# Retention values of two heads by seven products, with a DRAM round trip, and a reordered core sequence

## The chip, the cores and the metric

The kernel runs on one core of a Trainium2 chip. The metric is device time in microseconds (us) of one execution. TensorE does the matmuls, VectorE and ScalarE the elementwise work, GpSimd some of it, and SP, ScalarE and GpSimd issue DMA transfers.

## The reference

Two layers of a trunk: gated delta net with a convolutional FFN, then retention with the same FFN, each step closed by a layer norm. The change lies in the second layer's mixer, for 1024 tokens, 1024 features, 4 heads, keys of 256 and values of 512 per head, chunks of 128 tokens:

```python
def retention(h, w_in, w_out):
    H, dk, dv, C = RET_HEADS, RET_DK, RET_DV, RET_CHUNK          # 4, 256, 512, 128
    q, k, v, gate = jnp.split(h @ w_in, [H * dk, 2 * H * dk, 2 * H * dk + H * dv], axis=-1)
    ...                                                          # q, k rotated by position
    scores = jnp.einsum('bhncd,bhnmd->bhncm', q, k) * dmask[None, :, None]
    intra = jnp.einsum('bhncm,bhnmv->bhncv', scores, v)
    def step(state, inp):
        q_n, k_n, v_n = inp
        o = jnp.einsum('bhck,bhkv->bhcv', q_n, state) * xi[None, :, :, None]
        state = (state * gamma_c[None, :, None, None]
                 + jnp.einsum('bhck,bhcv->bhkv', k_n * zeta[None, :, :, None], v_n))
        return state, o
    _, inter = lax.scan(step, jnp.zeros((b_, H, dk, dv), F32), xs)
    o = _unchunk_heads(intra + jnp.moveaxis(inter, 0, 2))
    o = _standardize(o, 1e-6).reshape(b_, s, H * dv)             # each row of 512 to mean 0, variance 1
    o = o * jax.nn.silu(gate.astype(F32))
    return o.astype(h.dtype) @ w_out
```

## The kernel before

Most float32 matmuls are made of three: each operand is split into a high and a low part in a rounded format (`split`: ScalarE copies the high part, VectorE subtracts it for the low part), and low x high, high x low and high x high are added up in PSUM. One 128x512 result over 128 features is thus three matmuls (`mma`, `mm3`).

PSUM has eight banks of 128x512: four "acc", two "mm", two "sc". SBUF tiles come from tags with fixed numbers of buffers: "qkv" 20 (128x512 each), "aux", "cv" and "lane" 4, "auh" and "hTb" 8, "wr", "wh", "wl" and "xT" 2.

Big products run as Strassen-Winograd: the tokens (two halves) and features (two halves) of the activations give four blocks 11, 12, 21, 22 and four sums T1 to T4, and seven products of half size replace eight. `strassen` does so for the q, k and gate projections of the layer, and leaves its activation blocks (`B`) in SBUF: 11 and 21 in "hTb", T1 and 22 in "hTa", T2 in "aux", T3 and T4 in "qkv".

The value projection of each head, in the kernel before, is plain: `ret_v(h, half)` multiplies half the tokens (4 tiles of 128, one "acc" bank each) by 8 blocks of 128 features: 96 matmuls. It then splits each of the four results into a pair of "qkv" tiles, or waits for room there (`take`). It is called for head 0 halves 0 and 1, then head 1, and so on.

A core (`core(h)`) walks the 8 chunks of a head. Per chunk: two state products (kz by v, three matmuls each, into an "sc" bank, added to the state by VectorE), the next chunk's scores and key transposes (`ret_front`, "mm" bank), then the output product (scores by v, and q by state, "sc" bank). `ret_back` takes the output's statistics on VectorE, the power -0.5 on GpSimd, normalises the row (tile "on"), transposes it on TensorE, multiplies it with the gate loaded from DRAM ("gt", giving "ot") and stores it to DRAM (`od`), from chunk 4 on also in sums and differences with the earlier half ("op", made by GpSimd), as the output projection's blocks.

The output projection (`proj_gen`, started by `start_out`) is a seven-product scheme too; its first product reads eight blocks of `od`, two per head. Block j may start when the event `("ob", j // 2)` of head j // 2 stands, which is set after chunk 3 of that core; the last two blocks are the seventh and eighth, of head 3.

The order on TensorE in this stage is written by a planner (`run`): generators yield times to wait or events; the planner keeps a clock from the cost of each matmul, always advances the ready generator of lowest number, and pins the matmuls in that order. Cores have -1.0, `ret_back` -0.1, the filler `ret_fill` 0: it yields the value projection and then the first two products of the output projection, in groups of three matmuls, whenever no core is ready. The constants `RL` are the planner's latencies: "q" 5.9 us for loading q and k, "f" 3.35 after the first front, "p" 0.55, "c" 2.75 after an output product, "o" 4.42 from a transposed row to the output projection's block. Everything that is not pinned is placed by the framework's scheduler, each engine and queue running its instructions in order.

Of the kernel before, what the change touches and what calls it, by code (L numbers as in the profile page):

```python
# [15 lines left out]
P = 128  # L16
# [17 lines left out]
def trunk_kernel(ctx: ExitStack, tc, A):  # L34
# [1882 lines left out]
    B = strassen(h0, xts, sc_r, sh_r, [gate_item(0), gate_item(2)] + mixed, ("hTa", "aux", "qkv", "qkv", "hTa"), True)  # L1917
    hT = [h0, []]
# [7 lines left out]
    hT[1] = build_hT("hTa", xlo, sc_r, sh_r, range(4)) + B["22"]  # L1926

    def ret_v(h, half):
        accs = acc4()
        for kp in range(4):  # L1930
            wh, wl = load_w(A["ret_wv"][h, kp])
            if (h, half, kp) == (RH - 1, 1, 3):
                yield after_ev(("qk", h))
                start_out()
            for kk in range(2):
                kt = kp * 2 + kk
                hl = hT[half][kt]
                ns = slice(kk * 4, kk * 4 + 4)
                for t in range(4):
                    ts_ = slice(t * P, (t + 1) * P)  # L1940
                    pm(accs[t], hl[1][:, ts_], wh[:, ns], start=(kt == 0), stop=False)
                    pm(accs[t], hl[0][:, ts_], wl[:, ns], start=False, stop=False)
                    pm(accs[t], hl[0][:, ts_], wh[:, ns], start=False, stop=(kt == KT - 1))
                    yield 0.0
            if kp % 2 or h == RH - 1:
                bg_step()
        for t in range(4):
            yield from take("qkv", 2)
            vv = two("qkv", F32R, "vv")
            split(vv[0], vv[1], accs[t])  # L1950
            va[h].append(vv)
# [23 lines left out]
    def core(h):  # L1975
        yield after_ev(("rv", h, 0), ("core", h - 1))
        if h == 1:
            bg_ada(1, 2, "row")
        q, k = load_qk(h, 0), load_qk(h, 1)
        emit(("qk", h))  # L1980
        St = None
        yield RL["q"]
        r = ret_front(h, 0, q, k)
        yield RL["f"]
        for n in range(NCH):
            if n == 4:
                yield after_ev(("rv", h, 1))
            vh, vl = va[h][n]
# [25 lines left out]
            give("qkv", 2)  # L2014
# [3 lines left out]
        emit(("core", h))  # L2018

    def ret_back(h, n, po):  # L2020
# [9 lines left out]
        anchor["on"] = dve.tensor_scalar(on, po, mv[:, 0:1], mv[:, 3:4], ALU.subtract, ALU.mult)  # L2030
# [33 lines left out]

    def load_qk(h, j):
# [8 lines left out]
    RL = {"v": 2.57, "q": 5.9, "f": 3.35, "p": 0.55, "c": 2.75, "b": 3.21, "o": 4.42}  # L2074
    va = [[] for _ in range(RH)]

    def ret_fill():
        for h in range(RH):
            for half in range(2):
# [39 lines left out]
    run([(0.0, ret_fill())] + [(-1.0, core(h)) for h in range(RH)])  # L2119
# [104 lines left out]
```

## Time and profile before

| what | value |
|---|---|
| time, median of 3 runs (lowest, highest) | 2871.21 us (2867.52, 2874.64) |
| the profiled execution's own time, and its span | 2872.47 us, 2870.7 us |
| TensorE, VectorE, ScalarE, GpSimd busy over the span | 97%, 76%, 45%, 17% |
| granted TensorE clock | 0.994 |
| matmul records | 13594 |
| HBM read, written | 346.86 MB, 115.87 MB |
| DMA engines' mean rate | 162 GB/s |

In the lines below, a window's row gives the busy microseconds (and count) of TensorE matmul, its weight load, VectorE, ScalarE and GpSimd, then the granted clock, the DMA share and GB/s. A row of the chain gives start, duration and what the time went to. A matmul's duration includes its way through the pipeline; its cost in a dense stretch is the distance from one start to the next. In a timeline row, square brackets hold the engine's idle time ahead of the instruction and what ended it.

### The profile page before, as it was taken

Reading aid. Unit: us, or ns where it says so; the run is one execution under the profiler, and the core shown is the slowest. Engines: PE = TensorE matmul, PEld = TensorE weight load, DVE = VectorE, ACT = ScalarE, POOL = GpSimd, SP = SyncE. Lnnn points to the kernel's source line nnn. Section 1 sums busy time; section 2 is a strip of 40 time slices with the busy share of each in tenths; the row PEclk is TensorE's granted clock in tenths of the full one; section 3 lists DMA queues with packets and bytes.
Section 4 is the critical chain, followed back from the end, with each engine's and each line's share of the span. In section 5 each row is a group of like instructions: output and inputs, shape, how many; then the busy total and the mean of one; then the engine's idle time right before and its main releaser. Section 6 shows DMA issues by size and latency. Waiting matters only on the chain.

```text
span 2870.7 us, 38939 instructions
## 1 busy us (share of the span) xinstructions
PE 2785.2 (97%) x13594; PEld 2277.0 (79%) x13594; DVE 2183.3 (76%) x3874; ACT 1294.0 (45%) x2377; POOL 500.2 (17%) x517
## 2 busy tenths in 40 slices
PE   8999999999999999999999999999999999999997
PEld 6787878877787788887888887777787778888886
DVE  6887678676788888778677656666788887777869
ACT  3763465344644444546433342222344644444443
POOL 0411321000023233100000002333301033332001
PEclk9999999999999999999999999999999999999999
DMA  8323242174254555945343364665854253444853
GB/s 279 101 90 115 92 140 92 61 250 150 99 180 168 192 183 172 336 126 180 128 147 119 121 204 153 200 196 160 275 194 147 74 194 132 143 139 161 320 150 118
DMA packets 254292, 465.31 MB, mean 162 GB/s; under 512 B 24400, under 2 KB 81104, under 8 KB 254096
## 3 DMA queue, kind: packets, MB, share of 16 engines
q1 hardware_dynamic: 219776, 407.50, 43.0%
q10 hardware_dynamic: 31488, 46.15, 4.4%
q0 software_dynamic: 2832, 9.18, 0.8%
q8 instruction: 107, 1.75, 0.2%
q14 instruction: 89, 0.73, 0.1%
HBM read 346.86 MB, written 115.87 MB: 161 GB/s over the span
## 4 chain that ended last, share of the span: by engine, by line
PE 56%; DVE 21%; DMA 11%; ACT 6%; issue 5%; POOL 1%; SPq 0%; ACTq 0%; DVEq 0%; POOLq 0%
PE acc L747 10%; PE acc L1340 5%; PE acc L110 4%; PE sc L747 4%; PE acc L111 4%; PE acc L112 4%; PE sc L1340 3%; PE acc L1636 3%; DMA mvw<-in_ada_w 3%; DVE o L1787 3%; DMA wr<-in_ffn_up 2%; PE mm L747 2%; DVE wb L90 2%; DVE qkv L507 2%; DVE mm L1394 1%
## 5 line engine op out<-in xcount | busy, mean ns | idle before, releaser
L747 PE MATMUL acc<-hT,wh 128*128 128x512 f32 x960 | 299.7, 393 | 0.0
L1636 PE MATMUL acc<-bb,ab 128*128 128x512 f32 x984 | 229.8, 392 | 6.5 <-DVE ab L90 4.1
L89 ACT ACTIVATE ab<-ar 128x512 fp32r<-128x512 f32 x210 | 131.1, 629 | 217.0 <-PE mm L316 55.1
L1636 PEld LDWEIGHTS acc<-bb,ab 128*128 128x128 f32 x984 | 183.0, 188 | 48.6 <-DVE ab L90 4.7
L747 PEld LDWEIGHTS acc<-hT,wh 128*128 128x128 f32 x960 | 182.5, 190 | 35.6
L1340 PE MATMUL acc<-T,wb 128*128 128x512 f32 x840 | 202.0, 389 | 0.4 <-DVE wb L90 0.4
L90 DVE TENSOR_TENSOR ab<-ar,ab 128x512 fp32r<-128x512 f32 x210 | 148.7, 715 | 68.5 <-ACT ab L89 68.1
L747 PE MATMUL acc<-hT,wl 128*128 128x512 f32 x480 | 197.3, 411 | 1.2 <-ACT sq L531 0.7
L89 ACT ACTIVATE wb<-mm 128x512 fp32r<-128x512 f32 x216 | 124.4, 597 | 163.0 <-DVE mm L1394 150.1
L1340 PEld LDWEIGHTS acc<-T,wb 128*128 128x128 f32 x840 | 157.5, 188 | 33.8 <-ACT o L1788 1.1
L90 DVE TENSOR_TENSOR wl<-wr,wh 128x1024 fp32r<-128x1024 f32 x95 | 118.6, 1249 | 74.3 <-ACT wh L89 72.6
L1818 POOL TENSOR_TENSOR o<-o 128x512 f32<-128x512 f32 x80 | 119.0, 1496 | 270.1 <-DVE o L1810 167.9
L90 DVE TENSOR_TENSOR wb<-wr,wb 128x512 fp32r<-128x512 f32 x162 | 114.2, 706 | 65.7 <-ACT wb L89 65.6
L89 ACT ACTIVATE wh<-wr 128x1024 fp32r<-128x1024 f32 x95 | 100.6, 1060 | 138.3 <-PE acc L747 61.4
L1787 DVE SCALAR_TENSOR_TENSOR o<-g,vc,o 128x512 f32<-128x512 f32 (+2 forms) x176 | 152.2, 875 | 8.9 <-ACT o L1782 7.7
L90 DVE TENSOR_TENSOR wb<-mm,wb 128x512 fp32r<-128x512 f32 x216 | 144.5, 682 | 7.4 <-ACT wb L89 7.4
L89 ACT ACTIVATE wb<-wr 128x512 fp32r<-128x512 f32 x162 | 101.2, 626 | 95.5 <-PE acc L1340 28.8
L1394 DVE TENSOR_TENSOR mm<-wr 128x512 f32<-128x512 f32 x108 | 83.9, 777 | 71.4 <-DMA wr<-in_ffn_up 58.2
L747 PE MATMUL acc<-wh,hT 128*128 128x512 f32 x384 | 134.3, 412 | 2.1 <-DVE vv L90 2.1
L1410 ACT ACTIVATE pc<-acc 128x512 f32<-128x512 f32 x143 | 84.4, 591 | 111.8 <-PE acc L1340 63.6
L252 DVE SCALAR_TENSOR_TENSOR ada<-mvw,e,ada 128x512 f32<-128x512 f32 x140 | 105.8, 755 | 24.0 <-DMA mvw<-in_ada_w 23.8
L110 PE MATMUL acc<-T,wb 128*128 128x512 f32 x292 | 114.9, 394 | 3.6 <-DVE wb L90 3.3
(677 smaller groups left out, 7356.2 us busy)
## 6 DMA issues: line engine op xcount, KB each, us to landing
wr<-in_ffn_up SPq DMA_DIRECT2D x92, 512.0 KB, 3.9
mvw<-in_ada_w SPq DMA_DIRECT2D x80, 512.0 KB, 4.3
ad<-o SPq DMA_DIRECT2D x154, 256.0 KB, 2.3
ar<-ad SPq DMA_DIRECT2D x154, 256.0 KB, 4.2
Br<-in_ffn_down SPq DMA_DIRECT2D x88, 256.0 KB, 5.2
wr<-in_ret_wv SPq DMA_DIRECT2D x32, 512.0 KB, 3.6
ar<-od SPq DMA_DIRECT2D x56, 256.0 KB, 4.5
wr<-in_gdn_wqkv SPq DMA_DIRECT2D x24, 512.0 KB, 3.9
```

The lines of the kernel that those rows point to most:

```text
L89: anchor["sp"] = act.activation(dst_h, src, AF.Copy)
L90: eng.tensor_tensor(dst_l, src, dst_h, ALU.subtract)
L110: mm(acc, wl[:, k], hl[0], start=first, stop=False)
L111: mm(acc, wh[:, k], hl[1], start=False, stop=False)
L112: mm(acc, wh[:, k], hl[0], start=False, stop=last)
L252: dve.scalar_tensor_tensor(a, wr[:, kk], e[:, k:k + 1], a, ALU.mult, ALU.add)
L747: pq(pe.matmul(out, lhsT, rhs, start=start, stop=stop), cost or COST[out.shape[-1]])
L1340: return pe.matmul(*a, skip_group_check=True, **kw)
L1394: dve.tensor_tensor(t, x, y, op)
L1636: return pe.matmul(*args, skip_group_check=True, **kw)
L1787: dve.scalar_tensor_tensor(tv, gv[:, c0 - j:c1 - j], w[:, 2 - j:3 - j], tv, ALU.mult, ALU.add)
L1818: (dve if fp == 0 else pool).tensor_tensor(o[d], o[x], o[y], op)
```

## The change

Three things are changed.

1. Values of heads 0 and 1 are computed ahead of the planner's run by seven products (`values_01`) on the blocks that `strassen` left, and stored to DRAM (`vd`). During the run `fetch_v` loads them back at most two chunks ahead. The second half of the plain activations (`hT[1]`) is built inside this step.
2. The filler now holds only the values of heads 2 and 3, by token halves: both heads' first half, then both heads' second half; head 2's second half goes into "hTb". Core h + 1 starts after the event that core h now sets at chunk 6, and its q and k are loaded at chunk 5. The output projection's start waits for the event `("ob", 1)`.
3. The normalisation of each row moves from VectorE to ScalarE: VectorE makes minus mean times power (128x1), ScalarE scales and shifts.

```diff
+    def values_01():
+        W = A["ret_wv"]
...
+        def operand(p, j):
+            if p == 0:
+                src = first[j]
+            elif p == 1:
+                src = load(0, 1, j)
+            elif p == 2:
+                src = keep[j] = load(1, 0, j)
+                dve.tensor_tensor(src, src, load(1, 1, j), ALU.add)
+            elif p == 3:
+                src = keep[j]
+                dve.tensor_tensor(src, src, first[j], ALU.subtract)
...
+            t = tl(("wh", "wl")[(4 * p + j) % 2], [P, 2, HALF], F32R, name="wb")
+            split(t[:, 0], t[:, 1], src)
+            return t[:, 0], t[:, 1]
...
+        def put(h, n, c):
+            vv = two("qkv", F32R, "vv")
+            split(vv[0], vv[1], c)
+            for i in range(2):
+                act.dma_start(vd[h, n, i], vv[i].bitcast(F32))
...
+        for p, nm in enumerate(("11", "21", "T1", "T2", "22", "T3", "T4")):
+            fresh = p in (0, 1, 2, 6)
+            if p == 0:
+                X = acc4()
+            elif fresh:
+                Z = [sc_tile(), sc_tile(), mm_tile(), mm_tile()]
+            if p == 5:
+                hT[1] = build_hT("hTa", xlo, sc_r, sh_r, range(4)) + B["22"]
+            accs = X if p in (0, 3, 5) else Z
+            ws = []
+            for j in range(4):
+                while len(made) < min(4 * p + j + 4, len(steps)):
+                    made.append(operand(*steps[len(made)]))
+                ws.append(made[4 * p + j])
+                if j < 2:
+                    for t in range(4):
+                        mma(accs[t], t, B[nm][j], ws[j], fresh and j == 0, False, pe.matmul if fresh else mm_on)
+            if p in (0, 2, 3, 5):
+                part[p] = four("lane" if p == 2 else "xT")
+            for t in range(4):
+                for j in (2, 3):
+                    mma(accs[t], t, B[nm][j], ws[j], False, j == 3, pe.matmul if fresh else mm_on)
+                if p in part:
+                    act.activation(part[p][t], accs[t], AF.Copy)
+                if p in (1, 4, 5, 6):
+                    c = part[{1: 0, 4: 3, 5: 2, 6: 5}[p]][t]
+                    dve.tensor_tensor(c, accs[t], c, ALU.add)
+                    put(p // 5, t + (4 if p in (4, 5) else 0), c)
...
-    hT[1] = build_hT("hTa", xlo, sc_r, sh_r, range(4)) + B["22"]
+    values_01()
...
             if (h, half, kp) == (RH - 1, 1, 3):
-                yield after_ev(("qk", h))
+                yield after_ev(("ob", 1))
                 start_out()
...
         for t in range(4):
-            yield from take("qkv", 2)
-            vv = two("qkv", F32R, "vv")
+            if (h, half) != (2, 1):
+                yield from take("qkv", 2)
+            vv = two("qkv" if (h, half) != (2, 1) else "hTb", F32R, "vv")
...
     def core(h):
-        yield after_ev(("rv", h, 0), ("core", h - 1))
+        yield after_ev(("rv", h, 0) if h > 1 else ("vf", h, 0), ("core", h - 1))
         if h == 1:
             bg_ada(1, 2, "row")
-        q, k = load_qk(h, 0), load_qk(h, 1)
-        emit(("qk", h))
+        if not h:
+            qk[0] = load_qk(0, 0), load_qk(0, 1)
+            emit(("qk", 0), RL["q"])
+        q, k = qk[h]
         St = None
-        yield RL["q"]
+        yield after_ev(("qk", h))
         r = ret_front(h, 0, q, k)
         yield RL["f"]
         for n in range(NCH):
-            if n == 4:
+            if n == 5 and h < RH - 1:
+                qk[h + 1] = load_qk(h + 1, 0), load_qk(h + 1, 1)
+                emit(("qk", h + 1), RL["q"])
+            if n == NCH - 2:
+                emit(("core", h))
+            if n == 4 and h > 1:
                 yield after_ev(("rv", h, 1))
+            if h < 2:
+                yield after_ev(("vf", h, n))
...
-            give("qkv", 2)
+            if h != 2 or n < 4:
+                give("qkv", 2)
+            used[0] += 1
...
-        anchor["on"] = dve.tensor_scalar(on, po, mv[:, 0:1], mv[:, 3:4], ALU.subtract, ALU.mult)
+        dve.scalar_tensor_tensor(mv[:, 2:3], mv[:, 0:1], -1.0, mv[:, 3:4], ALU.mult, ALU.mult)
+        act.activation(on, po, AF.Identity, bias=mv[:, 2:3], scale=mv[:, 3:4])
...
+    def fetch_v():
+        for m in range(2 * NCH):
+            yield lambda: m < used[0] + 2
+            yield from take("qkv", 2)
+            vv = two("qkv", F32R, "vv")
+            for i in range(2):
+                sp.dma_start(vv[i].bitcast(F32), vd[m // NCH, m % NCH, i])
+            va[m // NCH].append(vv)
+            emit(("vf", m // NCH, m % NCH), RL["l"])
...
     def ret_fill():
-        for h in range(RH):
-            for half in range(2):
+        for half in range(2):
+            for h in range(2, RH):
                 yield from ret_v(h, half)
...
-    run([(0.0, ret_fill())] + [(-1.0, core(h)) for h in range(RH)])
+    run([(0.0, ret_fill()), (-2.0, fetch_v())] + [(-1.0, core(h)) for h in range(RH)])
```

More of the change, by code (lines that the diff above doesn't have):

```diff
@@ L2017, in core @@
             St, r = Sn, rn
-        emit(("core", h))
+        emit(("done", h))
     def ret_back(h, n, po):
@@ L2063, in ret_back @@
             (pool if n == NCH - 1 and h == RH - 1 else sp).dma_start(blk(nm), d)
+    used, qk = [0], {}
+    def fetch_v():
[7 more added lines that the diff above has]
+            emit(("vf", m // NCH, m % NCH), RL["l"])
     def load_qk(h, j):
@@ L2072, in load_qk @@
         return out
-    RL = {"v": 2.57, "q": 5.9, "f": 3.35, "p": 0.55, "c": 2.75, "b": 3.21, "o": 4.42}
+    RL = {"v": 2.57, "q": 5.9, "f": 3.35, "p": 0.55, "c": 2.75, "b": 3.21, "o": 4.42, "l": 4.0}
     va = [[] for _ in range(RH)]
     def ret_fill():
-        for h in range(RH):
-            for half in range(2):
+        for half in range(2):
+            for h in range(2, RH):
                 yield from ret_v(h, half)
```

27 lines of the change are left out of this document (added).

## The prediction

> **What bounds the kernel now.** I read the page's head first, then the stage that the change touches (from the last product of the input projections, 1702.3 us, to the end of the output projection's second product, 2082.0 us) by windows, then the chain of work in one chunk, then the rows of the operations that are added or removed.
>
> ```profile
> span 2870.7 us, 38939 instructions
> PE 2785.2 (97%) x13594; PEld 2277.0 (79%) x13594; DVE 2183.3 (76%) x3874; ACT 1294.0 (45%) x2377; POOL 500.2 (17%) x517
> ```
> ```profile
> 1640.00:1700.00 60.00, 59.44 (x262) 48.90 (x262) 43.55 (x69) 22.06 (x38) 0.00 (x0) 1.00 0.53 168
> 1702.30:2082.00 379.70, 371.79 (x1671) 287.64 (x1670) 242.59 (x430) 103.12 (x174) 119.54 (x132) 1.00 0.63 197
> 2020.00:2062.00 42.00, 39.95 (x176) 29.49 (x174) 28.61 (x58) 12.75 (x26) 12.48 (x17) 1.00 0.80 254
> ```
>
> TensorE bounds the kernel. The first window is the stage of seven-product input projections just ahead (TensorE 99%, VectorE 73%, ScalarE 37%), the second the stage of the change (98%, 64%, 27%), both at full clock. So a matmul taken away is worth its issue interval, as long as nothing else then runs out. One chunk of a retention core, from the chain that ended last:
>
> ```profile
> 1749.28 0.65 PE mm L750 x6
> 1749.93 0.69 PE acc L747 x3
> 1750.62 2.42 PE sc L747 x7
> 1753.04 3.44 PE acc L747 x15
> 1756.48 1.36 PE sc L747 x6
> 1757.84 0.44 PE mm L747 x4
> 1758.28 0.65 PE mm L750 x6
> ```
>
> The chunk takes 9.00 us. The "acc" pieces are filler (the value projection): 18 matmuls in 4.13 us, 0.229 each. The other 4.87 us are the core itself. Filler hides the core's waits, above all the one behind the 2.42 us output product: its rows must be normalised before their PSUM bank (two "sc" banks for all) takes the next chunk's second state product.
>
> ```profile
> 1753.08 0.70 DVE L2022 BATCH_NORM_STATS2 rst<-sc 128x6 f32<-128x512 f32 x1 [0.24 <-PE sc L747]
> 1754.91 0.81 DVE L2030 TENSOR_SCALAR on<-sc,mv 128x512 f32<-128x512 f32 x1 [0.73 <-POOL mv L2026]
> ```
>
> That is 1753.04 to 1755.72, 2.7 us, under 3.44 us of filler. What the change does to the amount of filler is therefore the question.
>
> **The change, part by part.**
>
> *Matmuls.* Values of heads 0 and 1 cost 2x2x8x4x3 = 384 matmuls; seven products of 4x4x3 = 48 cost 336. 48 x 0.229 = **-11.0 us**. The sixteen transposes for the second half of hT stay (moved to the sixth product).
>
> *Stalls that go.* In the old stage the filler has one set of four accumulators, drained between value halves with no core running beside it:
>
> ```profile
> 1728.08 0.62 issue
> 1728.70 0.69 DVE vv L90
> ...
> 1806.22 1.37 DVE vv L90 x2
> ...
> 1808.23 0.68 DVE vv L90
> ...
> 1810.05 0.61 DVE vv L90
> 1810.70 7.14 PE acc L747 x30
> 1818.50 3.43 PE acc L747 x15
> ...
> 1887.44 1.37 DVE vv L90 x2
> ...
> 1889.44 0.68 DVE vv L90
> ...
> 1891.17 0.69 DVE vv L90
> ...
> 1977.77 0.69 DVE vv L90
> ```
>
> The chain puts 7.4 us on these drains; TensorE still ran the old core's last products under part of them, so I count a little under half. The new stage alternates two sets of banks, and its four remaining drains fall inside chunks, where the core's own matmuls cover them: **-3.5 us** (bounds -7.4 and 0).
>
> *The new stage of seven products.* 76.9 us of TensorE. VectorE: 28 splits, 16 operand sums, 16 result sums, 16 value splits, 4 hT splits = 80 at 0.69 (the vv row) = 55 us, 72%; the first window runs 99% dense at 73%. ScalarE: 68 passes at 0.6, plus 32 stores issued at 0.33:
>
> ```profile
> 1651.09 0.33 ACTq L1899 DMA_DIRECT2D qd<-pc  x1
> ```
> ```profile
> L89 ACT ACTIVATE vv<-acc x32: 577/598/602, 1724.4 to 2012.2; 128x512 fp32r<-128x512 f32 x32
> ```
>
> That is 51 us, 67%, against 37% in that window, and every second store waits on ScalarE's queue for VectorE's low half, with the next operand's high half behind it. Operands are made four blocks ahead (four times 2.75 us), but only four "wb" buffers exist, so the lead is two blocks, 5.5 us. Also, only four of the twenty "qkv" buffers are free until T3 is spent, so the third value pair of the second product waits for the store of the first (3-4 us by the store rows below). Cost between 0.6 us (the first window's share of idle) and 6 us (two late operands of a lead lost); I take **+2**, nearer the window, which has the same structure. Weight loads fall (7 MB for 8), and 8 MB of stores with 8 MB of reloads come. At a DMA share of 0.5 to 0.6 they fit; the reloads stand on SP's queue some 12 us ahead of use by the two-chunk rule in fetch_v, priced at nothing; if SP stands still for over 12 us they show as a wait of "sc" matmuls for vv.
>
> *The order of the cores.* Now a core's q and k are loaded at chunk 5 and the next core starts at chunk 6. The old gap between cores held 30 + 15 filler matmuls (the rows at 1810 and 1818), 10.6 us. From core 1 on, the next core's first chunk now lies between the old one's last two (after core 0 it waits for the reloaded values). Both share two "sc" banks and two "mm" banks, and the second state product of the new core waits for the normalised row of the old one's chunk 6: 2.7 us less one filler group (0.69) and the first state product (0.68), 1.3 us. Then chunk 7's square products stand on GpSimd ahead of the new core's power:
>
> ```profile
> 1787.25 4.15 DMA od<-ot
> ...
> 1791.46 0.74 POOL ot L2062
> ```
> ```profile
> 1792.75 0.81 DVE L2030 TENSOR_SCALAR on<-sc,mv 128x512 f32<-128x512 f32 x1 [2.56 <-POOL mv L2026]
> ...
> 1813.45 0.69 DVE L2051 TENSOR_TENSOR ot<-mm,gt 128x512 f32<-128x512 f32 x1 [2.81 <-DMA od<-op]
> ```
>
> In this jam (a store, then GpSimd, then the row) the row waited 2.56 us in place of 0.73, 1.8 late against a slack of 1.4 (3.44 + 0.68 - 2.7): 0.4 us of TensorE, which stays. Two overlapped boundaries at 1.3, and one such 1.8 with no filler over it, make **+4** (bounds 0, where filler lies in between, and 3 x 4.15 = 12).
>
> *ScalarE normalises the row.* A 128x1 step on VectorE (0.15, as its neighbours) and a ScalarE pass (0.60) replace 0.81: 0.66 us per chunk off VectorE, 0.60 onto ScalarE, the row 0.1 to 0.2 us later through one more hand-over. Under 3.44 us of filler that is nothing; without filler it is 0.15 a chunk. ScalarE's queue now waits for GpSimd's power too, with kz and sThl behind it, as VectorE's did. The anchor "on" falls away with VectorE's row, and with it the order that holds the projection's T1 weight sums behind the last row:
>
> ```profile
> 2058.76 3.03 DVE L1515 TENSOR_TENSOR Bw<-Br,Bw 128x512 f32<-128x512 f32 x4
> ```
>
> They may now come earlier, ahead of rows or splits: bounds -3 and +3. Together **0**.
>
> *Filler.* The planner's order can be followed by hand from its own costs; a filler group is three matmuls. Groups there are: 128 (values of heads 2 and 3) and 24 (six of eight blocks of the output projection's first product), 152 in all, before its seventh block must wait for core 3's fourth chunk ("ob", 3). Used: 20 before core 0's first chunk, 46 from there to core 1's, 42 to core 2's second chunk, 30 for its chunks 1 to 5, 6 in the overlap, 6 in core 3's chunk 1: 150. **Filler ends in chunk 2 of core 3.** Before, 256 + 24 groups stood against the same cores, and the seventh block came late:
>
> ```profile
> 2025.87 0.60 PE L750 MATMUL mm<-cst,on 128*128 128x128 f32 x4
> ...
> 2046.87 4.00 PE L747 MATMUL acc<-bb,ab 128*128 128x512 f32 x15
> ```
>
> The first row turns row 3 of core 3; the seventh block begins in the second row, 21 us on, when its data had long been there. Now chunk 3 lacks 2.1 us of cover (2.8 to the released bank, less the first state product's 0.68), chunk 2 lacks 1.4 (one group is left). In chunk 4 the planner allows 4.42 us from the transposes of row 3 to the seventh block (the constant "o"), then puts its matmuls into TensorE's order ahead of chunk 5. Behind them on TensorE stand chunks 5 to 7. The true way is: product with the gate, store, load, split. (The other new wait, start_out behind ("ob", 1), is reached in core 2, when core 1's first half is long stored: 0.)
>
> ```profile
> od<-ot ACTq DMA_DIRECT2D x48, 128.0 KB, 3.6
> ...
> ar<-od SPq DMA_DIRECT2D x39, 256.0 KB, 5.3
> ```
> ```profile
> DMA to landing us min/median/max: 1.8/3.7/7.9
> ```
> ```profile
> DMA to landing us min/median/max: 2.7/5.3/7.9
> L89 ACT ACTIVATE ab<-ar x25: 615/632/634, 1996.4 to 2099.1; 128x512 fp32r<-128x512 f32 x25
> L90 DVE TENSOR_TENSOR ab<-ar,ab x24: 674/682/1227, 1997.0 to 2097.0; 128x512 fp32r<-128x512 f32 x24
> ```
>
> By medians 0.69 + 3.6 + 5.3 + 0.63 + 0.68 = 10.9 us; chunk 4's output product covers 2.4, so TensorE stands 8.5. By the shortest landings (1.8, 2.7) 6.5, so 4.1. Starved time: 1.4 + 2.1 + 4.1 to 8.5 = 7.6 to 12.0; I take **+10**, the middle: no value weights are loaded any more then, but the stretch has a DMA share of 0.80 (third window). The bounds are 0, if the cores reach this point with filler left, and 15, with the longest landing of the load (7.9).
>
> A page bears on the load and store. The Trainium skill, "DMA: Bandwidth & Descriptors", section "Anatomy of one DMA", gives about 2.0 us fixed plus bytes at 436 GB/s for transfers that GpSimd issues (these come from SP and ScalarE), an estimate here of 2.3 us for 128 KB and 2.6 us for 256 KB. By it the gap would be 4.5 in place of 8.5, starvation 8.0, and the sum -0.5 with that in place of +10. The trace's medians, 3.6 and 5.3, are longer than the page gives, so the rows carry the sum.
>
> *Sum.* -11.0 - 3.5 + 2 + 4 + 0 + 10 = **+1.5 us**. The profiled execution took 2872.47 us (span 2870.7), 1.3 above the median of 2871.21; so 2872.7 on the runs' scale. About 0.3% (8.6 us) is what a measurement of this kernel tells from no change.
>
> **The rivals.**
>
> *Faster: the filler suffices.* If core 3 is reached later in the filler's supply, or the seventh block's data come inside other work, starvation is 0 to 2 and boundaries 1. For it: TensorE was 98% dense with 18 matmuls a chunk, and the new run has exactly 576 = 32 x 18 filler matmuls. Against it: 120 of them are locked behind ("ob", 3). -11.0 - 3.5 + 2 + 1 + 1 = -10.5: 2861.
>
> *Slower: the ring of four "cv" buffers at the overlaps.* Chunk 7 of one core and chunk 0 of the next need op, gate row and result at once; VectorE stands at the result's product until a store has landed (2.81 in the row at 1813), now with a core behind it that has no filler. One store (3.6) and one such wait (2.81) at each of three boundaries are 19 us for my 4: +16.5, 2888. It decides (beyond 8.6) from 3.7 us per boundary. For it: the old gap of 10.6 us between cores cleared that ring, and it is gone. Against it: chunk 0 needs no op buffer.
>
> *The operands bind in the seven products.* Every second block late by 0.7 us on ScalarE's queue: 14 x 0.7 = 10 in place of 2: 2881. Against it stands the window ahead.
>
> **Chances.** Forecast 0.50; filler suffices 0.27; ring 0.15; operands 0.08. Forecast's own range 2865 to 2880. The first and third rival reach beyond 0.3% on their sides: faster 0.27, same 0.50, slower 0.23. The range takes the faster rival's centre and half of the slower ones: 2859 to 2884.
>
> **What would show it.** Right: 48 fewer matmuls; the seven products in about 79 us; TensorE's gaps in the last core, chunks 2 to 4, with its longest wait for the seventh block's split; rows from ScalarE at about 0.6 us; no wait of "sc" for reloaded vv. Wrong: filler still present in core 3's chunk 4; long gaps at the ends of cores 0 to 2; "wb" splits releasing TensorE in the seven products; or a time moved outside 1702 to 2082, where nothing is edited.

## The result, and the profile after

The changed kernel took 2888.48 us in the median of 4 runs (2885.99 to 2889.99), the kernel before 2870.24 beside it: a ratio of 1.0065, 95% interval 1.0048 to 1.0081. The change made the kernel slower by 18.7 us (the ratio times 2870; the medians differ by 18.2). Forecast was 2872.7, with a range of 2859 to 2884.

The head of the page of the changed kernel, then its windows (the columns are the stretch, its length, busy time and instructions of TensorE, weight loads, VectorE, ScalarE and GpSimd, the granted clock, DMA share and GB/s):

```profile
span 2887.1 us, 39162 instructions
PE 2781.2 (96%) x13546; PEld 2269.8 (79%) x13546; DVE 2188.2 (76%) x3918; ACT 1327.8 (46%) x2437; POOL 496.5 (17%) x517
...
1700.40:2098.80 398.40, 369.40 (x1624) 282.20 (x1624) 250.63 (x478) 135.53 (x233) 113.33 (x132) 0.98 0.72 232
...
1700.40:1780.00 79.60, 79.60 (x360) 65.96 (x360) 48.57 (x75) 41.60 (x69) 0.00 (x0) 1.00 0.62 214
...
1793.00:1820.00 27.00, 24.60 (x113) 18.60 (x112) 19.89 (x42) 8.22 (x15) 7.96 (x7) 1.00 0.93 318
1820.00:1864.00 44.00, 44.00 (x200) 33.32 (x199) 24.73 (x54) 13.29 (x23) 15.82 (x20) 1.00 0.75 245
1864.00:1886.00 22.00, 16.72 (x70) 13.21 (x69) 11.36 (x21) 4.21 (x7) 9.14 (x11) 0.84 0.80 234
1886.00:1920.00 34.00, 34.00 (x159) 26.52 (x158) 22.35 (x45) 11.02 (x18) 7.57 (x9) 1.00 0.80 251
1920.00:1958.00 38.00, 32.53 (x147) 23.21 (x146) 22.05 (x50) 9.85 (x17) 20.45 (x25) 1.00 0.75 225
...
1980.00:1996.00 16.00, 12.36 (x45) 8.20 (x44) 13.11 (x24) 5.89 (x11) 2.57 (x4) 0.89 0.77 263
1996.00:2022.00 26.00, 22.39 (x105) 16.05 (x104) 16.82 (x41) 7.98 (x15) 13.11 (x17) 1.00 0.59 170
2022.00:2040.00 18.00, 17.31 (x79) 12.90 (x78) 10.33 (x21) 3.46 (x6) 8.40 (x10) 1.00 0.58 177
2040.00:2060.00 20.00, 13.03 (x41) 8.21 (x40) 9.96 (x24) 6.08 (x11) 3.62 (x4) 0.84 0.71 223
2060.00:2098.80 38.80, 37.86 (x168) 29.07 (x167) 28.35 (x49) 14.60 (x27) 18.18 (x23) 1.00 0.80 251
```

The 48 matmuls are gone (13546 for 13594). The whole loss lies in the stage forecast: 398.4 us where the window of before had 379.7, that is +18.7. (Ahead of the stage the profiled execution is 1.9 us shorter than the one of before, and behind it 0.4, so the two spans are 16.4 us apart; runs of the kernel before alone differ by 7.) Take a window's length less TensorE's busy time as idle. The seven products (the second window) have none. The rest has 29.0 us, all in a few places: 2.4 as core 0 starts, 5.3, 5.5 and 3.6 at the three boundaries between cores (1864, 1920, 1996), 3.6 at 1980, and 0.7 + 7.0 + 0.9 in the last core. Before had 379.70 - 371.79 = 7.9 in all. The stretches between are dense at 44.00 of 44.00 and 34.00 of 34.00: cores with filler are as good as they were.

The clock is the other part. The records of the granted clock show half speed for 17.1 us of the stage (6.83 from 1876.0, 3.41 from 1988.6, 6.83 from 2053.5) against 3.4 before. What ran then took twice its time. TensorE stood idle in 2.0 us of the 17.1, so half of the 11.7 us more in which it worked is lost: 5.8. The account: -11.0 for the matmuls, +21.1 of idle time, +5.8 of clock are +15.9 of the 18.7. Most of the other 2.8 is a matter of counting: a matmul's record lasts 0.389 us and its cost is 0.229, so a gap takes 0.16 us more than its idle time. The stage has 22 gaps of over 0.25 us, and had 8 before; 14 times 0.16 is 2.2 us, an estimate. Counted with these 0.16, the gaps named below are 5.4 us (5.3 of idle time), 4.75 (4.6) and 2.1 (1.95).

Now the chain of waits at five of these places (start, duration, what): core 0's second chunk, the boundary of cores 0 and 1, the boundary of cores 1 and 2, core 2's modulations, and the seventh block of the output projection.

```profile
1794.77 8.29 DMA xg<-xs
...
1806.25 5.54 DMA xg<-xg
...
1811.89 0.70 DVE Sr L2098
...
1867.12 4.27 DMA xg<-xs
...
1871.56 1.24 POOL xg L2211
...
1874.66 0.72 POOL op L2161
1875.39 0.52 POOL mv L2124
...
1875.93 0.68 DVE mv L2128
...
1876.69 0.79 ACT on L2129
...
1877.53 1.65 PE sc L747 x3
...
1880.03 1.28 PE mm L750 x6
...
1944.10 2.79 DMA od<-op
...
1947.10 0.70 DVE ot L2150
...
1947.85 0.66 PE mm L750 x4
...
1981.05 4.67 DMA ar<-od
...
1986.40 0.69 DVE ab L90
...
1987.68 0.76 DVE ada L252
...
1988.58 2.00 PE mm L274 x2
...
2050.30 3.88 DMA ar<-od
...
2054.20 0.64 ACT ab L89
...
2054.87 0.70 DVE ab L90
...
2055.62 1.65 PE acc L747 x3
```

The second place is the largest gap of the stage. GpSimd's queue is in order. On it stand a gain row (the residual row times the layer's gain plus its bias, lines 2211 and 2212), whose load takes 4.27 us and keeps GpSimd waiting, then sums and differences of core 0's last chunks (L2161), and behind them the power (L2124) without which core 1's row can't be normalised. The row holds a PSUM bank, and TensorE stands 5.4 us. The rows after this gap show the clock: six transposes take 1.28 us, which took 0.65 at full clock before. The first place shows the same row by another way: core 0's state "Sr" takes a "lane" buffer that the gain row leaves only when its store has landed (5.54). The third place has no gain row on its chain: VectorE stands at the gated product until a store of "op" has landed (2.79), and transposes of TensorE stand behind it. That is the way of the prediction's second rival, the ring of "cv" buffers, which hold "op", "gt" and "ot".

The waits of GpSimd for these loads, in the kernel before (first row) and after (second row; engine, line, what it waited for: us, times, longest):

```profile
POOL xg L2100 <- DMA xg<-xs: 410.9, 15, 355.4
```
```profile
POOL xg L2211 <- DMA xg<-xs: 54.6, 15, 5.7
```

Before, one wait was 355.4 us, on an engine with nothing to do; the other fourteen make 55.5 us. After, all fifteen make 54.6. So the wait did not grow; the experiments ask whether its cost did.

### The profile page after: what moved, and what is told of

Its sections match the earlier page's. It is cut to its first block, busy times and chain, and to the rows that moved or that the text cites. A ratio compares the mean times of both kernels' runs of the same rounds, so it can differ in the third digit from the quotient of the medians.

```text
span 2887.1 us, 39162 instructions
## 1 busy us (share of the span) xinstructions
PE 2781.2 (96%) x13546; PEld 2269.8 (79%) x13546; DVE 2188.2 (76%) x3918; ACT 1327.8 (46%) x2437; POOL 496.5 (17%) x517
## 4 chain that ended last, share of the span: by engine, by line
PE 61%; DVE 18%; DMA 10%; ACT 5%; issue 4%; POOL 1%; SPq 1%; ACTq 0%; DVEq 0%; POOLq 0%
PE acc L747 7%; PE acc L1340 6%; PE acc L1636 4%; PE acc L110 4%; PE acc L111 4%; PE acc L112 4%; PE sc L1340 3%; PE sc L747 3%; PE mm L747 2%; DVE o L1787 2%; DVE qkv L507 2%; DMA mvw<-in_ada_w 2%; DMA wr<-in_ffn_up 2%; PE sc L110 2%; PE sc L112 2%
## 5 line engine op out<-in xcount | busy, mean ns | idle before, releaser
L1636 PE MATMUL acc<-bb,ab 128*128 128x512 f32 x984 | 230.3, 392 | 10.8 <-DVE ab L90 8.0
L1340 PE MATMUL acc<-T,wb 128*128 128x512 f32 x840 | 202.0, 389 | 0.4 <-DVE wb L90 0.4
L90 DVE TENSOR_TENSOR wl<-wr,wh 128x1024 fp32r<-128x1024 f32 x79 | 97.9, 1241 | 51.1 <-ACT wh L89 50.7
L89 ACT ACTIVATE wh<-wr 128x1024 fp32r<-128x1024 f32 x79 | 83.7, 1061 | 90.5 <-PE acc L341 47.3
L110 PE MATMUL acc<-T,wb 128*128 128x512 f32 x292 | 114.8, 393 | 2.9 <-DVE wb L90 2.8
L112 PE MATMUL acc<-T,wb 128*128 128x512 f32 x292 | 114.4, 392 | 0.0
```

The lines of the kernel that those rows point to most:

```text
L89: anchor["sp"] = act.activation(dst_h, src, AF.Copy)
L90: eng.tensor_tensor(dst_l, src, dst_h, ALU.subtract)
L110: mm(acc, wl[:, k], hl[0], start=first, stop=False)
L112: mm(acc, wh[:, k], hl[0], start=False, stop=last)
L1340: return pe.matmul(*a, skip_group_check=True, **kw)
L1636: return pe.matmul(*args, skip_group_check=True, **kw)
```

## The experiments

The theory at the start of them: the cores are short of cover in particular places (boundaries, starved last core), through waits that can be named. The rivals: the 8 MB of stores and reloads crowd the DMA queues; the row on ScalarE is too slow; the filler is short as such. Differences below are in ratios to the kernel before, which ran beside each; 0.001 is 2.9 us.

**One part undone at a time.**

```diff
-        dve.scalar_tensor_tensor(mv[:, 2:3], mv[:, 0:1], -1.0, mv[:, 3:4], ALU.mult, ALU.mult)
-        act.activation(on, po, AF.Identity, bias=mv[:, 2:3], scale=mv[:, 3:4])
+        anchor["on"] = dve.tensor_scalar(on, po, mv[:, 0:1], mv[:, 3:4], ALU.subtract, ALU.mult)
```


> The changed kernel with the row normalised by VectorE again (third part undone, its anchor back). Changed kernel: 2888.5 us; before: 2870.2. Theory 'row' (ScalarE took 0.78 us for a row and not 0.60, and one more hand-over, each chunk's bank later by 0.5 us wherever filler lacks): 2880 or less. Theories 'boundaries' and 'block' (the stalls come from the order of the cores and from the output projection's seventh block): 2886 to 2891.

2885.04 us, ratio 1.0042 (1.0027 to 1.0057), between the two expectations. By the ratios the row on ScalarE is worth 6.6 us of the 18.7, by the medians 3.4; the intervals of the two kernels overlap, so its price is not settled.

```diff
-            if n == NCH - 2:
-                emit(("core", h))
...
-        emit(("done", h))
+        emit(("core", h))
```


> The changed kernel with the next core released only after the old core's last chunk (q and k still loaded at chunk 5). Theory 'boundaries' (the three overlapped core boundaries lose 15 us beyond the old ones, on GpSimd's queue and the cv buffers): those stalls go, some 7 us come back because filler ends earlier in core 3; 2878 to 2883. Theory 'block' (what costs is the filler ending before the seventh block): no gain, 2888 to 2896.

The edit also finishes the modulations of layer 1 before the output projection starts (lines not shown). 2900.84, 1.0100 (1.0077 to 1.0123), above both expectations. Cores one behind the other are worse by 10 us by the ratios, with intervals that just touch: the overlap looks like a gain, though its boundaries have gaps.

```diff
-    RL = {... "o": 4.42, "l": 4.0}
+    RL = {... "o": 11.0, "l": 4.0}
```


> The changed kernel with one planner constant changed: the output projection's seventh block counts as ready 11.0 us after the row's transposes, not 4.42. Theory 'block' (TensorE's order holds the block's matmuls ahead of chunk 5, and they wait 4.8 + 0.7 us for data, and then run at half clock for 6.8 us): 2879 to 2883, and the longest gap of core 3 gone. Theory 'boundaries': 2886 to 2889.

2885.39, 1.0046 (1.0033 to 1.0060), between the two expectations, and its interval overlaps that of the changed kernel. The 4.75 us gap ahead of the seventh block is gone, but in the profiled execution the end of the stage gave back 6.3 of the 7.4 us won: from core 3's first output product to its last it took 58.8 us for 66.2, and from there to the end of the stage 27.8 for 21.5.

```diff
-            gains.pop(0)()
+            pass
...
-                            ... slots, xg[0], rows[1, 2], None,
+                            ... slots, xs[1], rows[1, 2], None,
```


> The changed kernel without the layer norm's gain and bias on the residual rows inside the cores (the output projection reads the rows without them): takes 34 products and 32 transfers of 256 KB off GpSimd and SP in cores 0 to 3. Theory 'gain' (GpSimd stands at these products for their loads, and the power of the next row behind them: gaps of 2.1 us at 1810 and 5.4 us at 1872): 2876 to 2881. Theory 'boundaries' by the cv buffers and the square products alone: 2885 to 2888.

2876.58, 1.0025 (1.0012 to 1.0037): 11.5 us better than the changed kernel, the largest step of any single edit, as the theory "gain" had it. The kernel leaves out a part of the computation, the gain and bias, so it shows a price and is no candidate. Its stage, then core 0's start and the three boundaries, with TensorE alone:

```profile
1694.60:2082.40 387.80, 366.33 (x1624) 280.46 (x1623) 246.88 (x479) 135.34 (x233) 71.72 (x100) 0.98 0.68 214
...
1787.30:1815.00 27.70, 26.92 (x125) 1.00 0.92 308
1855.00:1880.00 25.00, 24.19 (x114) 1.00 0.78 221
1905.00:1943.00 38.00, 33.88 (x153) 1.00 0.68 202
...
1980.00:2006.00 26.00, 22.88 (x106) 1.00 0.42 124
```

Idle falls from 29.0 to 21.5. Core 1 (first output product to the next core's) takes 63.1 us for 70.1. At the four places the idle time is 0.8, 0.8, 4.1 and 3.1 us, where the changed kernel has 2.4, 5.3, 5.5 and 3.6. So the gain rows make 8.0 of these 16.8 us, nearly all of the first boundary's; 8.8 us are there without them, most at the second and third boundary.

**Is it the amount of filler, or single buffers?**

```diff
+                    for rep in range(5 if (h, half, kt) == (3, 1, 0) else 1):
                         pm(accs[t], hl[1][:, ts_], wh[:, ns], ...)
```


> The changed kernel with the 48 matmuls that the seven products save put back as needless filler (the first block of head 3's second value half is computed five times over). Theory 'filler' (TensorE stands because too little filler is left for the cores, so a matmul taken out of this stage buys nothing): 2886 to 2892 against 2888.5, the gap of 4.8 us before core 3's fifth chunk smaller. Theory 'boundaries' (the stalls lie at places that filler does not reach): the full 11 us on top, 2898 to 2901.

2894.33, 1.0091 (1.0070 to 1.0111), between the two expectations. The 48 needless matmuls, 11.0 us of work, cost about 7 by the ratios, whose intervals overlap. If the filler's amount alone had been at fault they would have been free; they cover about 4 us, and the first boundary's gap is there as before (5.05 us of idle time at 1870).

```diff
-            x = tl("lane", [P, HALF], name="xg")
+            x = tl("xg", [P, HALF], name="xg")
```


> The changed kernel with one buffer of its own for the residual rows that get their gain on GpSimd (before: a share of the four 'lane' buffers, which hold the cores' states). Theory 'gain' (the row's load waits for a state's buffer, GpSimd waits for the load, and the next chunk's power stands behind it): the gaps of 2.1 us at 1810 and 5.4 us at 1872 go, with one stretch of 6.8 us at half clock; 2877 to 2882. If it is the transfers' own slowness and not the buffer: 2886 to 2889.

2892.41, 1.0086 (1.0069 to 1.0103), above both expectations. One buffer of their own for the gain rows is no gain. The first boundary's 5.3 us of idle time become 0.8, but 2.8 and 3.6 us come at the second, again with a gain row's load on the chain. That the rows wait for each other there, for the one buffer, is my reading and not tested.

```diff
-    RL = {... "c": 2.75, ...}
+    RL = {... "c": 2.7, ...}
```


> The changed kernel with one planner constant changed: 2.70 us in place of 2.75 after an output product. Four filler groups take 2.748 by the planner's costs, so 2.75 lets in a fifth; with 2.70 each chunk takes five groups in all and not six, and some 30 groups are left for core 3. Theory 'filler': 2876 to 2882, and no gap of over 3 us in core 3. Theory 'boundaries': 2886 to 2890, the gaps at the core boundaries as they were.

2887.48, 1.0069 (1.0054 to 1.0084), as the theory "boundaries" had it. Five filler groups a chunk in place of six last longer: core 3 no longer starves (from its output product of chunk 4, counted from 0, to that of chunk 5 it takes 8.3 us for 16.2), and the boundaries lose what it wins.

```diff
-    BUFS = {... "cv": 4, ...
+    BUFS = {... "cv": 5, ...
```


> The changed kernel with five 'cv' buffers in place of four. The slower rival of the prediction (VectorE waits at the gated row for a cv buffer whose store has not landed, at each overlapped boundary): the gaps between 1924 and 1955 and between 2000 and 2020 shrink by half, 2879 to 2884. Theories 'gain' and 'filler': 2886 to 2889.

2884.26, 1.0058 (1.0043 to 1.0073), at the edge of the rival's range. The ring of four "cv" buffers, the prediction's slower rival, is worth 2 us by the ratios, within the intervals. The idle time at the three boundaries falls from 14.4 to 12.5 us in its profile.

```diff
-  ... (ov[:, 1], ov[:, 1], pv[:, 0], ALU.subtract, "S3")):
+  ... (pair_view(g)[:, 1], ov[:, 1], pv[:, 0], ALU.subtract, "S3")):
```


> The changed kernel with GpSimd's last square sum of a chunk written over the spent gate row, so that it no longer waits for the store of the block whose buffer it overwrote (12.9 us of waits in the changed kernel's stage). Theory 'GpSimd' (its queue runs in order, and the row's power stands behind sums that wait for stores and gains that wait for loads; where two cores overlap nothing covers that): 2880 to 2884. Theory 'transfers' (8 MB of value stores and 8 MB of reloads make every landing later): 2886 to 2889.

2889.26, 1.0074 (1.0059 to 1.0090), and not the 2880 to 2884 of the theory "GpSimd". One wait of GpSimd for a store is gone, and the time stays.

**The transfers.**

```diff
-            for i in range(2):
-                act.dma_start(vd[h, n, i], vv[i].bitcast(F32))
+            act.dma_start(vd[h, n, 0], vv[0].bitcast(F32))
```


> The changed kernel storing and reloading only the high parts of the values of heads 0 and 1 and using them for the low parts too: 4 MB of stores and 4 MB of loads less, the matmuls the same. (The low parts of these values are left out.) Theory 'transfers': 2878 to 2883, the gaps of 2.1 and 5.4 us at the start of the run and after core 0 shorter by half. Theory 'GpSimd': 2885 to 2888.

The reload is halved in the same way. 2895.35, 1.0095 (1.0075 to 1.0114), above both expectations. Half of the stores and reloads bought nothing, so nothing speaks for the rival "transfers". Its half-clock time was 27.3 us for 17.1. Its profile has two new gaps of 2.7 us of idle time, one at 1802 behind passes of the modulations on VectorE, one at 1835 behind a gain row on GpSimd, and half speed follows both; why they came is not shown.

**The gain rows moved out of the cores.**

```diff
+                if gains:
+                    gains.pop(0)()
...
-        if n < 4 or h == RH - 1 and n == 4:
-            gains.pop(0)()
```


> The changed kernel with the residual rows' gain moved from the cores into the stage of the seven products, where GpSimd has no work at all; nothing is left out. Theory 'GpSimd': near the run without the gain, 2876 to 2880. Theory 'transfers': the same 8 MB now stand beside the value stores, and that stage, dense until now, gets stalls of its own; 2886 to 2894.

One step now stands after each operand of the seven products. 2891.40, 1.0077 (1.0058 to 1.0096), in the range of "transfers". The cores run 10.8 us shorter, as without gain rows (core 1 takes 63.1), but the first core matmul comes 104.9 us into the stage, not 92.7. The edit moved the loss.

> The changed kernel with five edits together: gains ahead, the square sum elsewhere, the row normalised by VectorE, five cv buffers, and the second layer's output gate vector begun in core 0 and not in core 1 (its VectorE passes wait for weights: 4 us of TensorE between 1982 and 1989). Theory 'GpSimd': 2864 to 2870, no slower than before. Theory 'filler' (what is left of the stalls is too little cover, wherever the waits lie): 2874 to 2880.

This is the edit of the last one with those of S3, the row and "cv", and the modulations begun in core 0 (`if h == 0: bg_ada(1, 2, "row")`). 2889.94, 1.0078 (1.0060 to 1.0095), far above both expectations. The modulations' gap in core 2 went (from chunk 4 to 5 it took 9.0 us for 16.0), and the seven products lost 16.0 us.

**The control, and all the named waits at once.**

> The kernel before, with the gain and bias of the residual rows left out of the cores (the output projection reads the plain rows). It is the control for the same edit on the changed kernel, which took 11 us off it. If the gain rows cost the changed kernel time because its cores have less filler over them, this kernel keeps its time: 2867 to 2872 us. If the gain rows cost the same with full filler, it falls by 8 to 11 us, to about 2860, and they are no reason for the loss.

2869.00, 1.0002 (0.9991 to 1.0013). The edit that took 11.5 us off the changed kernel takes nothing off the kernel before. That fits what the wait rows said: the gain rows' waits were there all along, and cost nothing under 18 filler matmuls a chunk and 45 at each boundary. The edit takes the rows' transfers away together with their waits; that it is the waits rests on the chain at 1867 above.

> The changed kernel with all the waits named so far taken away together: the gain and bias of the residual rows left out, S3 written into the gate tile, the row normalised by VectorE, five cv buffers, the layer's row of modulations in core 0, and the seventh block's planned way at 11.0. Theory 'four waits of the cores' (gain, modulations, seventh block, boundary buffers): idle time of TensorE in the stage falls from 29 to 10 us or less and the half clock to 7 us or less, so 2859 to 2866. Rival 'the filler is short': the gaps move to other places, idle stays at 18 us or more, 2872 or more.

2867.44, 0.9999 (0.9987 to 1.0010). All 18.7 us of loss are gone, in a kernel that leaves out gain and bias too. The stage and the chain where the seventh block stood:

```profile
1697.20:2074.80 377.60, 362.72 (x1623) 279.71 (x1623) 265.08 (x478) 111.61 (x201) 75.70 (x100) 0.99 0.69 218
```
```profile
2044.10 1.39 PE acc L747 x6
2045.49 2.40 PE sc L747 x7
2047.90 3.45 PE acc L747 x15
2051.35 2.41 PE sc L747 x7
```

Idle is 14.9 us, half clock 6.8. I had expected 10 or less and 2859 to 2866: the waits account for the loss, but not for the gain that should then have been left. Apart from the gain rows, what each of the six edits is worth is not separated by this run. 7 us of idle more than before (14.9 against 7.9) stay, in gaps of 0.3 to 1.6 us at the boundaries and in the last core's chunks, and one of 3.6 where core 1 begins, a place that is slow in all the runs that begin the modulations in core 0. These 7 and 1.7 of clock (half of 6.8 - 3.4) eat most of the 11.0.

**Can the loss be brought back with the whole computation in place?**

```diff
-            sp.dma_start(xg[0][rs, hs(c)], x)
+            pool.dma_start(xg[0][rs, hs(c)], x)
...
```


> The changed kernel with the gain steps moved ahead into the seven products, as before, but their loads and stores issued from GpSimd's queue in place of SP's. Theory 'SP's queue': in the earlier run the operands' loads stood on SP behind a gain row's store that waits for GpSimd; now the stage of seven products is dense again (first core matmul at 93 to 96 us after the start of the stage, 104.9 then) and the cores keep their 11 us: 2877 to 2881. Rival 'VectorE is slowed': its splits took 0.85 us in place of 0.69 beside GpSimd's passes; then 102 us or more to the first core matmul and 2887 to 2892.

This is on top of the edit that moved the gain rows out of the cores, and the gain steps' loads move with the store. 2897.16, 1.0098 (1.0083 to 1.0114), above both ranges, with the first core matmul at 104.0 for 104.9. So SP's queue was not the cause. What the operands' passes waited for, in this kernel, by the rows of the tile "vr" (the changed kernel has 7.5, 3 there):

```profile
  DMA vr<-in_ret_wv: 18.9, 8
```

> Gains ahead from GpSimd's queue, S3 into the gate tile, the row on VectorE, five cv buffers, the modulations in core 0 and the seventh block's planned way at 11.0, with the whole computation. Theory 'SP's queue' and 'four waits': as the run with the waits taken away, plus 3 us at most: 2862 to 2870. Rival 'VectorE is slowed' or 'the filler is short': 2880 or more.

2884.39, 1.0054 (1.0035 to 1.0074), in the rival's range. Its cores are as short as those of the run with the waits taken away (core 3 takes 55.5 us, there 55.6), and its seven products take 15.7 us longer.

```diff
-                gbs.append([tl("auh", [P, HALF], name="gb") for _ in range(2)])
+                gbs.append([tl("t2", [P, HALF], name="gb") for _ in range(2)])
```


> As the run with the gains ahead from GpSimd's queue, but the gain and bias rows stand in the 't2' buffers, which the seven products leave unused, in place of four of the eight 'auh' buffers, through which the operands' loads pass (four more of those hold the kept sums). Theory 'the auh ring': the loads of vr come early again and the first core matmul stands at 93 to 97 us, not 104; the time is 2877 to 2882. Rival 'VectorE is slowed by GpSimd's passes' (a split took up to 1.76 us beside them): 101 us or more, and 2888 or more.

This is on top of the kernel of 2897.16. 2906.28, 1.0140 (1.0121 to 1.0160), the slowest; the first core matmul came at 116.3. The gaps of the second and third product went, as the theory of the "auh" ring has it (the run is dense to 1739), but one of 3.8 us of idle time follows there and one of 14.3 at 1750:

```profile
PEld sc L1946 <- ACT vc L2022: 14.7, 1, 14.7
ACT vc L2022 <- POOL xg L1925: 12.5, 1, 12.5
```

The products' partial results and the gain rows share the "lane" buffers, and the gain and bias of the second column half came late through the three "t2" buffers. Place and time are on the side of the rival, but this gap is neither theory's.

> As before with the gains ahead from GpSimd's queue and S3, the row, five cv buffers, the modulations and the block's planned way together, now with the gain and bias rows in 't2'. Theory 'the auh ring': the 15.7 us that the seven products lost there (108.4 against 92.7 to the first core matmul) come back but for 0 to 4 us, 2868 to 2874, at the kernel before. Rival 'VectorE is slowed': 2880 or more.

2891.53, 1.0086 (1.0071 to 1.0100), in the rival's range, with the same gap (13.9 us at 1748). No version with the whole computation beat the kernel before; the nearest is the one with its row on VectorE. Whether the gain rows have any place where they are free stays open: each that I tried took a buffer from the operands' loads, then one from the results.

## Why the prediction was wrong, by its own steps

**Matmuls, -11.0.** Right in number and rate, since the stretches with cover are dense.

**Stalls that go, -3.5.** Too large. In the old stage TensorE waited 2.1 us in all for splits of values, in four waits, and not the 7.4 that the chain puts on them; the rest of its 7.9 us of idle time had other causes. The account below still sets all 7.9 against all 29.0, as old and new places differ.

**Seven products, +2.** Measured 0 (79.60 of 79.60). VectorE was busy 61% there, for the 72% that I had worked out. ScalarE's 52% are without the issue of its stores; with 32 of them at 0.33 us it has 65%, for my 67%. So VectorE had more room than I thought, ScalarE as little, and it sufficed. The rival that put its price here falls.

**The order of the cores, +4. This is the step that failed.** The three boundaries have 14.4 us of idle time and core 0's start 2.4 more, where I had counted 4 in all: 16.8 us. I priced a boundary by the wait of a product for its normalised row and by sums on GpSimd in the way, and read a jam of 2.56 us from a row of before. I left out the rest of that queue: a gain row with its wait for a load stands on it in the first half of each core, which is now where the old core's end lies as well. The rows of GpSimd's waits in before showed 55.5 us of such waits, and I did not ask what covered them. By the run without gain rows they make 8.0 of the 16.8 us. The other 8.8 are still twice my price, mostly at the second and third boundary, where the chain shows rows and gated products behind GpSimd's sums, stores and loads; which of these is worth how much stays open. My range for the step (0 to 12) did not hold it either.

**The row on ScalarE, 0.** It took longer than estimated, 0.78 us in place of 0.60 (the row gives least, median and most in ns):

```profile
L2129 ACT ACTIVATE on<-sc,mv x32: 757/778/782, 1799.9 to 2083.8; 128x512 f32<-128x512 f32 x32
```

I took 0.60 from a plain copy of that size. Its price is what it adds to a boundary's chain: by the first experiment 3 to 7 us, not settled.

**Reloads, priced at nothing.** That held: the products that use the values never waited for a load, as their longest waits show (tile "vv": what its engine sat idle for, us, times), and halving the transfers was no gain.

```profile
  ACT on L2129: 24.1, 22
  DVE Sr L2098: 10.9, 10
  PE acc L747: 6.5, 6
```

**Starved filler, +10.** Right in place, and near in size. The filler of heads 2 and 3 did end early in core 3, and the largest gap comes between its chunks 4 and 5, behind store, load and split of the seventh block: 0.7 + 7.0 = 7.7 us in the chunks that I named, 0.9 at the core's end, and 3.2 of half clock (6.83 us from 2053.5, less 0.5 of idle time, halved). The load landed in 3.88 us, between the shortest (2.7) and the median (5.3) that I had taken.

**Left out: the modulations.** Their last reduction (the matmuls of line 274) falls in core 2 in both kernels. In the changed one it stands on VectorE behind a split whose block of the output projection lands after 4.67 us (the chain at 1981): 3.6 us of idle time and 1.7 of clock. They had a price before too, which I overlooked: there a pass of theirs waits for its weights, a row's statistics stand behind it on VectorE, and TensorE stands idle 2.0 us (at 1938.6), with 3.41 us at half speed after it. The chain of before:

```profile
1930.98 5.92 DMA mvw<-in_ada_w
...
1939.69 0.82 DVE on L2030
...
1940.56 1.65 PE sc L747 x3
```

So this place grew by 1.6 us of idle time.

**Left out: the clock, +5.8.** I took full clock throughout. Gaps of 5.4 and 4.75 us, and two near 1985 (1.1 and 2.4), were each followed by half speed for one or two times 3.41 us. The chain showed it at 1877 to 1882. The Trainium skill, "TensorE: Matmul & The Clock Gate", section "Part 1: The HAM clock gate (the "warmup" mystery)", says that a window of about 3.4 us spent idle halves the clock, by windows that run freely. The lengths here agree with it. The idle time does not: less than 3.4 us of it was enough near 1985, and 1.99 us in the kernel before.

By these terms: -11.0 - 7.9 + 2.4 + 14.4 + 3.6 + 8.6 + 5.8 + 2.8 (not assigned but for the estimate above) = +18.7.

**The rivals.** The ring of "cv" buffers gave 2888 and the right place, 6.4 us at each boundary where 5.3, 5.5 and 3.6 were measured. That its time fitted is luck: the first boundary's gap is a gain row's, a fifth buffer took back 2 us, and the rest of the 18.7 lies elsewhere and in the clock. Its wait, VectorE at a gated product until a store has landed, does stand on the chain of the second boundary. The filler did not suffice: the last place in the chain above shows the seventh block in the way.

## What to carry to other kernels

Before filler work is taken away or moved, list every wait that it covers now, on all engines and with its length, not only those of the engine that ends last. A wait that costs nothing today falls due when its cover goes. Taking the gain rows out was worth nothing before the change and 11.5 us after it. An in-order queue that mixes side work waiting for memory (the gain rows) with a step on the critical chain (the power) is the first place to look. And a gap of some microseconds on TensorE is to be priced with the half clock behind it, here about a quarter on top (5.8 for 21.1).

## What the runs showed of the hardware that I had not expected

A two-input VectorE pass slows beside GpSimd's passes. The split of an operand in the seven products, in the changed kernel, where GpSimd is idle, and with the gain rows there (least, median, most in ns):

```profile
L90 DVE TENSOR_TENSOR wb<-vr,wb x24: 684/692/694, 1704.5 to 1771.1; 128x512 fp32r<-128x512 f32 x24
```
```profile
L90 DVE TENSOR_TENSOR wb<-vr,wb x19: 675/685/1780, 1716.9 to 1771.9; 128x512 fp32r<-128x512 f32 x19
```

Most keep 0.69 us and some take up to 1.78. The four that take over 1 us all run beside a gain row's pass on GpSimd; those with no such pass beside them take 0.69 or less. The Trainium skill, "GPSIMD Engine Reference", section "Key points", says that GpSimd shares its way into SBUF with VectorE and that passes with two SBUF inputs contend; the trace agrees, and shows what it comes to: two and a half times the duration in the worst case.

Half clock came in whole steps of 3.41 us in this stage. A gap of about 2 us can go either way: 1.99 us of idle time brought 3.41 us of half speed in the kernel before (at 1938.6), 2.04 at the same place of the same kernel without gain rows brought none, and 1.95 (at 1810) in the changed kernel brought none.
